# Gate sums over partitions on Pool instead of TensorE, and a changed order on VectorE in the seven-product pairs

## The chip, the cores and the metric

The kernel runs on one core of a Trainium2 chip. The core has TensorE (PE, with its weight loads PEld), VectorE (DVE), ScalarE (ACT), GpSimd (Pool) and SyncE (SP), which here issues the loads; 16 DMA engines move data between HBM and the core's memory. The metric is the device time of one execution in microseconds (us), the median of several runs.

## The reference

One layer of a decoder trunk on 256 tokens of width 2048, all in float32. With x the tokens and c one conditioning vector:

```
shift, scale, gate = split(silu(c) @ ada_w + ada_b, 3)      # each 2048 wide
h = rmsnorm(x, norm_g) * (1 + scale) + shift
b_gate, c_gate, v, g = split(h @ w_in, 4)                   # each 4096 wide
u = causal_depthwise_conv(c_gate * v, conv_w)               # width 3
y = (b_gate * u * silu(g)) @ w_out                          # back to 2048
out = rmsnorm(x + gate * y, final_g)
```

The change is in the gate, a vector-matrix product over 2048 rows of ada_w, and in the last product, with w_out.

## The kernel before, in words

**Precision and loads.** Each weight tile of 128 x 2048 (1 MB) is loaded by SP. ACT casts it to the matrix format (the high part, `hi`, L341), DVE subtracts that from the original (the low part, `lo`, L346), and TensorE makes three products of each pair of operands: hi with hi, hi with lo, lo with hi (L471 for w_in, L695 for w_out). Raw, high and low tiles have three buffers each, which take turns.

**Stages.** First x is turned and normalised. Then blocks of four output tiles of w_in (`part`, `mm_s`) run while the shift and scale are still being made, with an order that a planner (`plan`) fixes. `mixed` does the convolution and the gating for each of four such chunks (L528 to L537). From about 381 us on, the second half of the 4096 columns runs in eight wider blocks (L626, `mm_b`), each of four parts, two tiles to a part. Last come the products with w_out: the first 1024 output columns from 730.79 us (L748, `mm_w` and `mm`), then two blocks of 512 (L790, `mm_o`).

**The gate.** For each of four groups of 512 output columns (`dc`), DVE multiplies 16 tiles of ada_w with silu(c) and accumulates them into `gacc`, 128 partitions by 512 (L591, L593). `gacc` uses the tag `gv`, which has two buffers, so a group takes the buffer of the group two before. At the end of a group a TensorE product with a matrix of ones sums over the partitions and puts the same sum in each (`ps_gate`, L596, float32 in two passes), and DVE adds the bias to it (L597). The bias was loaded into `gate` before (L563). Pieces of the gate are called once for each weight tile of the wide blocks, but with a later priority, so that a scheduler places them where it finds room.

**Token forms and pairs of seven products.** Six of the 16 pairs of row tiles of w_out (`SEVEN`, pairs 10 to 15) are multiplied with seven block products instead of eight, the Strassen-Winograd way. `token_forms` (L604) makes four sums of the blocks of y in a scratch half of `zs[0]` and keeps their high and low parts. `seven` (L713) does the same for the four 512-wide blocks of a raw tile: DVE makes the sums (L720, L722, L723) and the low part of the blocks themselves (L724), ACT casts the blocks (L721) and then the sums (L341), and DVE makes the sums' low part (L346). Between two such pairs stands an ordinary pair of 24 products, since the order of the pairs is (0, 1, 10, 2, 11, 3, 12, 4, 13, 5, 14, 6, 15, 7, 8, 9).

**What sets the order.** Each engine takes its instructions in the order of the built program. A scheduler makes that order from priorities and its own estimates of durations; `later` and `behind` shift or fix places, and `add_manual_dep` with `after` orders two instructions of one engine without a wait.

Of the kernel before, what the change touches and what calls it, by code (L numbers as in the profile page):

```python
# [8 lines left out]
F32 = mybir.dt.float32  # L9
F32R = mybir.dt.float32r  # L10
AF = mybir.ActivationFunctionType
ALU = mybir.AluOpType

P = 128
# [103 lines left out]
def short_conv_layer(ctx: ExitStack, tc: tile.TileContext, x, c, norm_g, ada_w, ada_b, w_in, conv_w, w_out, final_g, out):  # L118
    nc = tc.nc
# [11 lines left out]
    psum = ctx.enter_context(tc.tile_pool(name="psum", bufs=3, space=PSUM))  # L131
# [5 lines left out]
    def slot(shape, name, dtype=F32):  # L137
        return slots.tile(shape, dtype, tag="slot", name=name)
# [6 lines left out]
    def w_tile(kind, name, dtype=F32, i=None):  # L145

        if i is None:
            i = nth[kind] % 3
            nth[kind] += 1
        return wpool.tile([P, SLOT], dtype, tag=f"{kind}{i}", name=name, bufs=1)  # L150
# [12 lines left out]
    after = mybir.DependencyInfo(mybir.DependencyClass.NoSync, mybir.DependencyReason.DATA)  # L163
# [75 lines left out]
    ones = const.tile([P, 1], F32, tag="ones", name="ones")  # L239
# [35 lines left out]
    for t in range(TT):  # L275
        for dh in range(2):
# [3 lines left out]
            else:  # L280
                nc.vector.scalar_tensor_tensor(
                    out=junk[:, t], in0=xt[t][dh], scalar=1.0, in1=xt[t][dh], op0=ALU.mult, op1=ALU.mult,
# [50 lines left out]
    def hi_tile():  # L333
        return w_tile("hi", "hi", F32R)

    def lo_tile(lo_tag="lo"):
        return w_tile(lo_tag, "lo", F32R)
# [23 lines left out]
    def split(raw, n, lo_tag="lo"):  # L361

        return split_lo(raw, n, split_hi(raw, n), lo_tag)
# [64 lines left out]
    sums = {}  # L428
# [132 lines left out]
    zs = [slot([P, 2, 2, T], f"z{j}") for j in range(2)]  # L561
# [6 lines left out]
    def gate(dc):  # L568
        return gates[dc // 2][:, dc % 2, :]

    gate_todo = [(dc, j) for dc in range(4) for j in range(0, KT, 2)]
    gacc = [None]

    def gate_piece():
        if not gate_todo:
            return
        dc, j = gate_todo.pop(0)
        at = adap.tile([P, ASLOT], F32, tag="at", name="at_g", bufs=4)
        at3 = at.rearrange("p (k f) -> p k f", k=2)
        with later(GIVE):  # L580
            gate_sums(dc, j, at3)

    def gate_sums(dc, j, at3):
        nc.sync.dma_start(at3, adas[:, j : j + 2, 2, dc * 512 : (dc + 1) * 512])
        if j == 0:
            gacc[0] = adap.tile([P, 512], F32, tag="gv", name="gacc")
        ga = gacc[0]
        for i in range(2):
            s = silu_c[:, j + i : j + i + 1]
            if j + i == 0:  # L590
                nc.vector.tensor_scalar_mul(ga, at3[:, i, :], s)  # L591
            else:
                nc.vector.scalar_tensor_tensor(out=ga, in0=at3[:, i, :], scalar=s, in1=ga, op0=ALU.mult, op1=ALU.add)  # L593
        if j + 2 == KT:
            ps = psum.tile([P, 512], F32, tag="sm", name="ps_gate", bufs=2)
            nc.tensor.matmul(ps, ones.to_broadcast([P, P]), ga, start=True, stop=True)  # L596
            nc.vector.tensor_tensor(out=gate(dc), in0=ps, in1=gate(dc), op=ALU.add)  # L597

    KP = 8
    EP = 4  # L600
# [2 lines left out]

    def token_forms(pair, u):  # L604

        sums = zs[0][:, 0].rearrange("p a (b f) -> p (a b) f", f=P)
        a11, a12 = u[:, 0, 0:P], u[:, 1, 0:P]
        a21, a22 = u[:, 0, P:T], u[:, 1, P:T]
        s1n, s2, s3, s4 = (sums[:, j] for j in range(4))
        nc.vector.scalar_tensor_tensor(out=s1n, in0=a21, scalar=-1.0, in1=a22, op0=ALU.mult, op1=ALU.subtract)  # L610
        nc.vector.scalar_tensor_tensor(out=s2, in0=s1n, scalar=-1.0, in1=a11, op0=ALU.mult, op1=ALU.subtract)
        nc.vector.tensor_tensor(out=s3, in0=a11, in1=a21, op=ALU.subtract)
        nc.vector.tensor_tensor(out=s4, in0=a12, in1=s2, op=ALU.subtract)
        if pair < 14:
            form = adap.tile([P, ASLOT], F32R, tag="at", name="form", bufs=4).rearrange("p (h s f) -> p h s f", h=2, f=P)
            hi, lo = form[:, 0], form[:, 1]
        elif pair == 14:
            hi, lo = (adap.tile([P, 512], F32R, tag="gv", name="form_g").rearrange("p (s f) -> p s f", f=P) for _ in range(2))
        else:
            form = hpool.tile([P, 2, 4, P], F32R, tag="big2", name="form_h")  # L620
            hi, lo = form[:, 0], form[:, 1]
        forms[pair] = hi, lo
        nc.scalar.copy(hi, sums)
        nc.vector.tensor_tensor(out=lo, in0=sums, in1=hi.bitcast(F32), op=ALU.subtract)

    for ct in range(NS, NCT, 2):  # L626
        for q in QUARTERS:
# [17 lines left out]
            if q == 1:  # L645
                nc.scalar.copy(z, bank)
                zc = z
            elif q == 2:
                nc.vector.tensor_tensor(out=zc, in0=bank, in1=zc, op=ALU.mult)
                for j in range(2):  # L650
                    conv(ct + j, z[:, j, :], zc[:, j, :])
                u = z
            elif q == 3:
                nc.scalar.activation(z, bank, AF.Silu)
                nc.vector.tensor_tensor(out=u, in0=u, in1=z, op=ALU.mult)
            else:
                nc.vector.tensor_tensor(out=u, in0=bank, in1=u, op=ALU.mult)
                split_y(ys[ct // 2], u)
                if ct // 2 in SEVEN:
                    token_forms(ct // 2, u)  # L660
# [28 lines left out]
    def y_parts(ct, t):  # L689
        return [ys[ct // 2][:, ct % 2, h, t * P : (t + 1) * P] for h in range(2)]  # L690

    def triple(dst, y, hi, lo, opens=False, ends=False):

        for i, (a, b) in enumerate(((0, hi), (0, lo), (1, hi))):
            nc.tensor.matmul(dst, y[a], b, start=opens and i == 0, stop=ends and i == 2, skip_group_check=True)  # L695
# [17 lines left out]
    def seven(j, raw):  # L713


        opens, last = j == SEVEN[0], j == SEVEN[-1]
        sums = w_tile("lo", "sums_o")
        hi, lo = hi_tile(), lo_tile("raw")
        b, s, bh, bl = (v.rearrange("p (b f) -> p b f", f=W) for v in (raw, sums, hi, lo))
        nc.vector.tensor_tensor(out=s[:, 0:2], in0=b[:, 1:3], in1=b[:, 0:1].to_broadcast([P, 2, W]), op=ALU.subtract)  # L720
        nc.scalar.copy(bh[:, 1:4], b[:, 1:4])  # L721
        nc.vector.tensor_tensor(out=s[:, 2], in0=b[:, 2], in1=s[:, 0], op=ALU.add)  # L722
        nc.vector.tensor_tensor(out=s[:, 3], in0=b[:, 3], in1=s[:, 2], op=ALU.subtract)  # L723
        nc.vector.tensor_tensor(out=bl[:, 1:4], in0=b[:, 1:4], in1=bh[:, 1:4].bitcast(F32), op=ALU.subtract)  # L724
        sh, sl = (v.rearrange("p (b f) -> p b f", f=W) for v in split(sums, SLOT, "raw"))

        def f(i):
            return [forms[j][h][:, i] for h in range(2)]

        triple(p1, y_parts(2 * j, 0), bh[:, 1], bl[:, 1], opens, last)  # L730
        triple(wide[0][:, 1], y_parts(2 * j + 1, 0), bh[:, 3], bl[:, 3])
        triple(wide[0][:, 0], f(3), bh[:, 2], bl[:, 2])
        triple(p75[:, 0], f(2), sh[:, 1], sl[:, 1], opens, last)
        triple(p75[:, 1], f(0), sh[:, 0], sl[:, 0], opens, last)
        triple(p6, f(1), sh[:, 2], sl[:, 2], opens, last)
        triple(wide[1][:, 1], y_parts(2 * j + 1, 1), sh[:, 3], sl[:, 3])
# [12 lines left out]
    for n, j in enumerate(order):  # L749
        raw = w_tile("lo" if n else "raw", "raw_o")  # L750
        load_o(raw, 2 * j, 2, 0, 2 * W)
        load_ends(n - 4)
        if j in SEVEN:
            seven(j, raw)
            if j == SEVEN[-1]:
                gather()
            continue
        hi, lo = split(raw, SLOT, "raw")
        for t in range(TT):
            for k in range(2):  # L760
                for d in range(2):
                    o = slice((k * 2 + d) * W, (k * 2 + d + 1) * W)
                    triple(
                        wide[t][:, d], y_parts(2 * j + k, t), hi[:, o], lo[:, o],
                        n == 0 and k == 0, j == order[-1] and k == 1,
                    )
# [24 lines left out]
    for dc in range(2, 4):  # L791
# [16 lines left out]
        for ep in range(n_ep):  # L808
# [3 lines left out]
            if dc == 3:  # L812
# [3 lines left out]
                    out=raw3, in0=raw3, in1=gate(dc).unsqueeze(1).to_broadcast([P, EP, W]), op=ALU.mult  # L816
# [8 lines left out]
        for t in range(TT):  # L825
# [4 lines left out]
            if dc == 2:  # L830
                gated(t, dc * W, W, po[t], pr, 1)
                ps = part_sum[:, t : t + 1]
# [29 lines left out]
```

## Time and profile before

| | us |
|---|---|
| median of 3 runs | 911.48 (911.47 to 912.15) |
| the profiled execution | 911.95 |
| its span, first to last instruction | 910.2 |
| granted TensorE clock, mean | 0.997 of full speed |

The profiled execution is one run of its own; what lies between its time and its span is before the first and after the last instruction. Durations in the next parts come from it. In the lines of the profile, `out<-in` are the program's names, `xN` a count, and a number in brackets the idle time of the engine ahead of the instruction with what ended it. "hi L341 <- PE mm_b: 154.0, 46, 4.4" in a list of waits reads: waited for that, 154.0 us in total, 46 times, 4.4 us at the longest. A DMA's line gives its count, size and the us from issue to landing. In a table by stretches, x counts instructions.

### The profile page before, as it was taken

The numbers are of one execution on the slowest core, as the hardware profiler recorded it, in microseconds if no ns is written. First come the engines' busy times: TensorE is split into PE (matmuls) and PEld (weight loads), VectorE is DVE, ScalarE is ACT, GpSimd is POOL, SyncE is SP. The second block draws the span as 40 slices with busy tenths as digits, with TensorE's granted clock in tenths as the row PEclk, the third lists the DMA queues.
The fourth block names the chain that finished last, engine by engine and source line by source line (L and its number), as shares of the span: only waits on it lengthen the run. The fifth ranks groups of instructions, "written<-read, shape, count | busy, mean of one in ns | idle before, by whom it ended". The sixth has DMA issues, their size and how long they took to land.

```text
span 910.2 us, 16272 instructions
## 1 busy us (share of the span) xinstructions
PE 894.2 (98%) x7029; PEld 854.7 (94%) x7029; DVE 653.5 (72%) x647; ACT 476.1 (52%) x422; POOL 0.7 (0%) x6
## 2 busy tenths in 40 slices
PE   6999999999999999999999999999999999999996
PEld 4999999999999999999999999999999987788885
DVE  4889899889888886665555686555555577887882
ACT  6768866665558765643333434343444335544343
POOL 0000000000000000000000000000000000000000
PEclk9999999999999999999999999999999999999998
DMA  9999999999998686676666887656666486685542
GB/s 313 367 371 349 364 309 365 346 370 359 345 327 282 184 301 189 189 241 202 202 186 186 259 273 231 201 185 194 185 193 197 137 307 191 209 293 185 185 138 93
DMA packets 159656, 227.65 MB, mean 250 GB/s; under 512 B 5680, under 2 KB 104160, under 8 KB 159200
## 3 DMA queue, kind: packets, MB, share of 16 engines
q1 hardware_dynamic: 159456, 226.56, 75.7%
q8 instruction: 55, 0.90, 0.4%
q14 instruction: 17, 0.14, 0.0%
q10 hardware_dynamic: 128, 0.04, 0.0%
HBM read 224.49 MB, written 2.10 MB: 249 GB/s over the span
## 4 chain that ended last, share of the span: by engine, by line
PE 98%; ACT 1%; DMA 1%; ACTq 0%; issue 0%; DVE 0%
PE mm_b L471 38%; PE mm_s L471 38%; PE mm_o L695 10%; PE mm_w L695 7%; PE mm L695 2%; PE tp_idle L258 1%; DMA rows<-in_ada_b_dram 1%; PE sum L380 1%; PE ps_gate L596 0%; PE tp_g L461 0%; PE tp_x L310 0%; ACT hi L341 0%; ACT acc L492 0%; ACT hT L327 0%; ACT mm_s L504 0%; ACT big L787 0%
## 5 line engine op out<-in xcount | busy, mean ns | idle before, releaser
L471 PE MATMUL mm_s<-hT,hi 128*128 128x256 f32 x2048 | 350.4, 277 | 0.1
L471 PE MATMUL mm_b<-hT,hi 128*128 128x256 f32 x2048 | 349.4, 276 | 0.0
L471 PEld LDWEIGHTS mm_s<-hT,hi 128*128 128x128 f32 x2048 | 308.5, 188 | 1.0 <-ACT hT L327 0.3
L471 PEld LDWEIGHTS mm_b<-hT,hi 128*128 128x128 f32 x2048 | 308.2, 188 | 0.5 <-issue 0.5
L471 PE MATMUL mm_b<-hT,lo 128*128 128x256 f32 x1024 | 282.6, 276 | 0.0
L471 PE MATMUL mm_s<-hT,lo 128*128 128x256 f32 x1024 | 282.2, 277 | 0.0
L346 DVE TENSOR_TENSOR lo<-raw,hi 128x2048 fp32r<-128x2048 f32 (+1 forms) x66 | 148.0, 2243 | 113.6 <-ACT hi L341 113.2
L341 ACT CAST hi<-raw 128x2048 fp32r<-128x2048 f32 (+1 forms) x66 | 123.7, 1874 | 193.9 <-PE mm_b L471 152.6
L471 PEld LDWEIGHTS mm_b<-hT,lo 128*128 128x128 f32 x1024 | 192.2, 188 | 0.5 <-issue 0.5
L471 PEld LDWEIGHTS mm_s<-hT,lo 128*128 128x128 f32 x1024 | 191.7, 188 | 0.3 <-DVE lo L346 0.2
L346 DVE TENSOR_TENSOR lo<-raw_s,hi 128x2048 fp32r<-128x2048 f32 (+1 forms) x80 | 147.6, 1850 | 32.8 <-ACT hi L341 32.0
L341 ACT CAST hi<-raw_s 128x2048 fp32r<-128x2048 f32 (+1 forms) x80 | 124.0, 1559 | 72.9 <-PE mm_s L471 59.6
L454 DVE SCALAR_TENSOR_TENSOR gv<-at,silu_c,gv 128x512 f32<-128x512 f32 x105 | 78.6, 749 | 6.3 <-DMA at<-in_ada_w_dram 4.5
L341 ACT CAST hi<-raw_o 128x2048 fp32r<-128x2048 f32 x26 | 49.6, 1906 | 60.6 <-PE mm_o L695 36.6
L695 PE MATMUL mm_o<-hi,y 128*128 128x512 f32 x256 | 78.7, 389 | 0.0
L346 DVE TENSOR_TENSOR lo<-raw_o,hi 128x2048 fp32r<-128x2048 f32 x26 | 59.5, 2290 | 24.2 <-ACT hi L341 24.1
L492 ACT COPY acc<-mm_s 128x1024 f32<-128x1024 f32 x54 | 54.6, 1012 | 34.7 <-PE mm_s L471 34.7
L695 PE MATMUL mm_w<-hi,y 128*128 128x512 f32 x184 | 58.2, 390 | 0.0
L695 PEld LDWEIGHTS mm_o<-hi,y 128*128 128x128 f32 x256 | 48.0, 188 | 9.9
L695 PE MATMUL mm_o<-lo,y 128*128 128x512 f32 x128 | 49.5, 389 | 0.0
L593 DVE SCALAR_TENSOR_TENSOR gacc<-at_g,silu_c,gacc 128x512 f32<-128x512 f32 x60 | 45.0, 749 | 5.6 <-DMA at_g<-in_ada_w_dram 4.6
L695 PEld LDWEIGHTS mm_w<-hi,y 128*128 128x128 f32 x184 | 34.5, 188 | 7.7 <-ACT hi L341 0.2
(142 smaller groups left out, 512.6 us busy)
## 6 DMA issues: line engine op xcount, KB each, us to landing
raw<-in_sc_w_in_dram SPq DMA_DIRECT2D x64, 1024.0 KB, 5.6
raw_s<-in_sc_w_in_dram SPq DMA_DIRECT2D x47, 1024.0 KB, 8.5
raw_o<-in_sc_w_out_dram SPq DMA_DIRECT2D x32, 1024.0 KB, 5.1
at<-in_ada_w_dram SPq DMA_DIRECT2D x114, 256.0 KB, 8.4
raw_s<-in_sc_w_in_dram SPq DMA_DIRECT2D x33, 512.0 KB, 6.9
at_g<-in_ada_w_dram SPq DMA_DIRECT2D x32, 512.0 KB, 7.6
at<-in_ada_w_dram SPq DMA_DIRECT2D x6, 512.0 KB, 9.4
x<-in_x_dram SPq DMA_DIRECT2D x4, 512.0 KB, 6.1
```

The source lines that it names most:

```text
L258: nc.tensor.matmul(tp_idle, ident, ones[:, 0:1].to_broadcast([P, 512]), start=True, stop=True)
L341: nc.scalar.copy(hi[:, :n], raw[:, :n])
L346: nc.vector.tensor_tensor(out=lo[:, :n], in0=raw[:, :n], in1=hi[:, :n].bitcast(F32), op=ALU.subtract)
L380: nc.tensor.matmul(sums0[:, o * P : (o + 1) * P], rows[:, o // NK0, (o % NK0) * P : (o % NK0 + 1) * P], col.to_broadcast([P, P]), start=k ...
L454: nc.vector.scalar_tensor_tensor(out=gv, in0=at4[:, i], scalar=c_k, in1=gv, op0=ALU.mult, op1=ALU.add)
L471: mm = last_mm[0] = nc.tensor.matmul(dst, w, h[k], start=begins and left, stop=ends, skip_group_check=True)
L492: nc.scalar.copy(acc[ch, q], bank)
L593: nc.vector.scalar_tensor_tensor(out=ga, in0=at3[:, i, :], scalar=s, in1=ga, op0=ALU.mult, op1=ALU.add)
L695: nc.tensor.matmul(dst, y[a], b, start=opens and i == 0, stop=ends and i == 2, skip_group_check=True)
```

## The change

The product with ones and the addition behind it go. In their place Pool makes the sums over partitions in seven steps, with a shift `away` of 64, 32, 16, 8, 4, 2 and 1 partitions. In each step two DMAs that Pool issues copy `gacc`, turned around by `away` partitions, into `turned`, and Pool adds the copy to `gacc`. After the seven steps each partition holds the sum of all 128; Pool then adds the bias. `turned` is the first half of `zs[0]`, which held the sums of `token_forms`; these move to the second half, which also holds the block's first part.

In `seven`, the low part of the raw blocks is ordered behind the fourth sum on DVE.

```diff
     gate_todo = [(dc, j) for dc in range(4) for j in range(0, KT, 2)]
     gacc = [None]
+    turned = zs[0][:, 0].rearrange("p a f -> p (a f)")
...
         if j + 2 == KT:
-            ps = psum.tile([P, 512], F32, tag="sm", name="ps_gate", bufs=2)
-            nc.tensor.matmul(ps, ones.to_broadcast([P, P]), ga, start=True, stop=True)
-            nc.vector.tensor_tensor(out=gate(dc), in0=ps, in1=gate(dc), op=ALU.add)
+            away = 64
+            while away:
+                nc.gpsimd.dma_start(turned[0 : P - away], ga[away:P])
+                nc.gpsimd.dma_start(turned[P - away : P], ga[0:away])
+                nc.gpsimd.tensor_tensor(out=ga, in0=ga, in1=turned, op=ALU.add)
+                away //= 2
+            nc.gpsimd.tensor_tensor(out=gate(dc), in0=ga, in1=gate(dc), op=ALU.add)
...
-        sums = zs[0][:, 0].rearrange("p a (b f) -> p (a b) f", f=P)
+        sums = zs[0][:, 1].rearrange("p a (b f) -> p (a b) f", f=P)
...
-        nc.vector.tensor_tensor(out=s[:, 3], in0=b[:, 3], in1=s[:, 2], op=ALU.subtract)
-        nc.vector.tensor_tensor(out=bl[:, 1:4], in0=b[:, 1:4], in1=bh[:, 1:4].bitcast(F32), op=ALU.subtract)
+        all_sums = nc.vector.tensor_tensor(out=s[:, 3], in0=b[:, 3], in1=s[:, 2], op=ALU.subtract)
+        low = nc.vector.tensor_tensor(out=bl[:, 1:4], in0=b[:, 1:4], in1=bh[:, 1:4].bitcast(F32), op=ALU.subtract)
+        tc.add_manual_dep(low.ins, all_sums.ins.name, after, reason="the sums' cast runs beside the low part")
```

In the changed file the lines behind the first edit stand one to six further down: the gate's products are at L592 and L594, Pool's transfers at L598 and L599, its additions at L600 and L602; in `seven` the sums are at L725, L727 and L728, the cast at L726 and the low part at L729.

## The prediction

> **What bounds the kernel now.** I read the profile page first, its busy line and its chain of work that ended last; then the chain in order of time; then who waits for whom; then the timelines of the two stages that the change touches.
>
> ```profile
> PE 894.2 (98%) x7029; PEld 854.7 (94%) x7029; DVE 653.5 (72%) x647; ACT 476.1 (52%) x422; POOL 0.7 (0%) x6
> ...
> PE 98%; ACT 1%; DMA 1%; ACTq 0%; issue 0%; DVE 0%
> ```
>
> Busy time alone would prove little, but the chain agrees: 98% of the span is a chain of TensorE work. The other engines have room, Pool nearly all of it. So a TensorE instruction that goes is worth its full time, wherever the next product's operands are early. The waits of ACT between 400 and 730 us say that they are:
>
> ```profile
> ACT hi L341 <- PE mm_b L471: 154.0, 46, 4.4
> ```
>
> ACT waits 154.0 us in 46 places for TensorE to give back a buffer; no row of that view has it wait for a weight load. The chain in order of time (start, length, what) shows the sums that go, and the rate of the 512-column products:
>
> ```profile
> 302.94 1.72 PE ps_gate L596 x4
> ...
> 541.79 0.86 PE ps_gate L596 x2
> ...
> 586.20 0.86 PE ps_gate L596 x2
> ...
> 730.79 10.89 PE mm_w L695 x48
> ...
> 815.93 86.83 PE mm_o L695 x383
> ```
>
> All four sums stand on the chain, in two passes each. An undisturbed product takes 86.83 / 383 = 0.2267 us. The stage of the output's first half is the one place where TensorE is slower than that:
>
> ```profile
> 730.79:815.93 85.14, 85.11 (x368) 68.23 (x368) 66.95 (x52) 40.31 (x25) 0.00 (x0) 1.00 0.71 247
> ...
> PEld mm L695 <- DVE lo L346: 1.4, 4, 0.3
> PEld mm L695 <- ACT hi L721: 1.1, 4, 0.3
> ```
>
> The first row is the busy time of each engine in that stretch (PE, PEld, DVE, ACT, POOL, then the granted clock, 1.00, and DMA). The code has ten ordinary pairs of 24 products there and six seven-product pairs of 21, 366, and one hoisted from the next stage: 367 x 0.2267 = 83.20. So 85.14 - 83.20 = 1.94 us are lost, with weight loads waiting four times each for a low part and for a block's cast.
>
> **Part 1, the gate's sums.** Removed: 8 passes of TensorE on the chain, 1.72 + 0.86 + 0.86 = 3.44 us, and four additions on DVE that are off the chain. It would be less if the products behind a sum found their operands late once they come that much sooner; it cannot be more. How early operands are is in these rows (DVE's low part, ACT's casts):
>
> ```profile
> 437.17 2.29 DVE L346 TENSOR_TENSOR lo<-raw,hi 128x2048 fp32r<-128x2048 f32 x1 [3.15 <-ACT hi L341]
> ...
> 446.06 1.91 ACT L341 CAST hi<-raw 128x2048 fp32r<-128x2048 f32 x1 [3.53 <-PE mm_b L471]
> ...
> 451.54 1.92 ACT L341 CAST hi<-raw 128x2048 fp32r<-128x2048 f32 x1 [2.77 <-issue]
> ```
>
> The low part that ends at 439.46 belongs to the tile that TensorE begins when it gives a buffer back at 446.06: 6.6 us early, so I take all 3.44. The raw buffer free at 439.46 is cast again, three tiles on, at 451.54: 12.1 us for a load.
>
> Added: for each of four columns seven steps of two Pool DMAs and one Pool addition, then the gate's addition: 56 DMAs, 32 Pool instructions. Nothing else stands on Pool behind its 6 instructions of setup, so its waits queue only its own chain. The question is who waits for Pool. In the built program that is DVE's first product of the third and of the fourth column (L592 of the changed file: its accumulator is the buffer of two columns before) and, far later, the forms of pair 14. The third column's products have moved on DVE behind the first wide block's split at L424, the fourth's stand where they stood; four 0.5 MB loads move with them on SP, past some twenty weight loads and the gate's two bias loads, into a stage with time to spare on DVE (20.21 of 40 us busy) and on the DMA engines (0.63). The rows give the deadlines:
>
> ```profile
> 440.00:480.00 40.00, 40.00 (x356) 40.00 (x355) 20.21 (x15) 16.46 (x12) 0.00 (x0) 1.00 0.63 191
> ...
> 315.92 0.69 DVE L535 TENSOR_TENSOR acc<-acc,acc 128x512 f32<-128x512 f32 x1
> ...
> 396.10 1.29 DVE L597 TENSOR_TENSOR gate<-ps_gate,gate 128x512 f32<-128x512 f32 x2 [4.44 <-DMA gate<-in_ada_b_dram]
> ...
> 428.46 0.68 DVE L424 TENSOR_TENSOR y<-z,y 128x512 fp32r<-128x512 f32 x1
> ...
> 519.19 0.49 DVE L591 TENSOR_SCALAR gacc<-at_g,silu_c 128x512 f32<-128x512 f32 x1 [2.40 <-DMA at_g<-in_ada_w_dram]
> ...
> L593 DVE SCALAR_TENSOR_TENSOR gacc<-at_g,silu_c,gacc x60: 743/751/754, 223.7 to 545.4; 128x512 f32<-128x512 f32 x60
> ...
> L623 ACT CAST form_g<-z x1: 616/616/616, 689.5 to 689.5; 128x512 fp32r<-128x512 f32 x1
> ```
>
> The first column's chain starts when L535 frees the slot that holds the turned copy, about 316 us; its last addition needs the gate's bias, landed at 396.1. It must be done by 429: 113 us for seven steps, 16 us each. The second runs from 397 to a deadline of 519: 17 us a step. The fourth starts when its products end, about 546, and must give its buffer to a form of pair 14 at 689: 20 us a step. A step is not in the trace; the nearest rows bound it:
>
> ```profile
> 1.01 0.29 POOL masks.py:199 TENSOR_SCALAR_AFFINE_SELECT ident<-ident 128x128 f32<-128x128 f32 x1
> ...
> rows<-in_c_dram ACTq DMA_DIRECT2D x1, 8.0 KB, 3.2
> ...
> gate<-in_ada_b_dram SPq DMA_DIRECT2D x2, 512.0 KB, 10.9
> ```
>
> Pool's 128 columns in 0.29 us make 512 in 1.2 us; a DMA lands after 3.2 us at the least and 10.9 at the most. So a step lies between 4.4 and 12.1 us, and I take 6, as its transfers (at most 254 KB) are nearer to the small one. Seven take 42, at most 85 us: in time, and the gate itself is first used behind 815.93. Cost on the chain: 0. If that cover is gone, it is rival B.
>
> The Trainium skill speaks against this in "SBUF — State Buffer", section "Who interferes with whom": a DVE instruction with two SBUF inputs and a GpSimd instruction that reads SBUF exclude each other, and the later one waits for all of the other. No row of this profile can show that, since Pool is idle beside DVE. By it, an addition would hold up a low part by its own length; by the Pool row that is 1.2 us against the 6.6 of slack, so the sum stays the same, but a step grows.
>
> Also hidden: the forms' sums move to the half of the buffer that ACT overwrites for the next block; ACT and DVE have read it by then in their own order, two casts ahead.
>
> **Part 2, the low part behind the fourth sum.** One period of DVE (start, length) and its ACT partner:
>
> ```profile
> 756.59 1.22 DVE L720 TENSOR_TENSOR sums_o<-raw_o 128x1024 f32<-128x1024 f32 x1
> 757.72 1.75 DVE L724 TENSOR_TENSOR lo<-raw_o,hi 128x1536 fp32r<-128x1536 f32 x1
> 759.39 0.69 DVE L722 TENSOR_TENSOR sums_o<-raw_o,sums_o 128x512 f32<-128x512 f32 x1
> 760.11 0.69 DVE L723 TENSOR_TENSOR sums_o<-raw_o,sums_o 128x512 f32<-128x512 f32 x1
> 762.85 2.29 DVE L346 TENSOR_TENSOR lo<-sums_o,hi 128x2048 fp32r<-128x2048 f32 x1 [2.05 <-ACT hi L341]
> 765.06 2.29 DVE L346 TENSOR_TENSOR lo<-raw_o,hi 128x2048 fp32r<-128x2048 f32 x1
> 767.26 1.22 DVE L720 TENSOR_TENSOR sums_o<-raw_o 128x1024 f32<-128x1024 f32 x1
> ...
> 760.91 1.91 ACT L341 CAST hi<-sums_o 128x2048 fp32r<-128x2048 f32 x1 [4.05 <-DVE sums_o L723]
> ...
> 766.11 1.48 ACT L721 CAST hi<-raw_o 128x1536 fp32r<-128x1536 f32 x1 [1.49 <-DMA raw_o<-in_sc_w_out_dram]
> ```
>
> From L720 to L720 DVE takes 767.26 - 756.59 = 10.67 us, 2.05 of them idle until ACT has cast the sums. TensorE needs for the same two pairs 45 x 0.2267 = 10.20. So DVE, though busy only 79% of the stage, sets the pace: 0.47 us a period, four periods, 1.9 us. That is the 1.94 again.
>
> Now the 1.75 us of L724 move behind L723, into the 2.05 us of idleness. DVE's period becomes 10.67 - 1.67 = 9.0. What is late next? The load: the raw block is read last by L724, then at 1.13 + 0.72 + 0.72 + 1.75 = 4.3 us after L720; from the block's release to the next cast it was 766.11 - 760.80 = 5.3; together 9.6 us. ACT's three casts take 1.91 + 1.90 + 1.48 = 5.3. All are below 10.20, so TensorE becomes the bound. The block's low part is ready 4.3 us after L720, at 756.59 + 4.3 = 760.9, and the chain has its product at 762.65, so that this is early too:
>
> ```profile
> 762.65 0.45 PE mm L695 x2
> ```
>
> In the built program four pairs also have their first product, which waited for L721, some 23 places later. Gain between 0 (the load binds after all) and 1.94; I take 1.9, as each loop above has 0.6 us to spare.
>
> **The sum.** 3.44 + 1.9 = 5.34 us. The profiled execution took 911.95 us, of which the span is 910.2; it would take 906.6. The median is 911.48, 0.47 below it: **906.1 us**.
>
> **Rivals.**
> A. Only the TensorE passes count: the stage stays at 85.1 us because the load is the loop. For it: ACT waits 1.49 us for the load in the row above. Against: that wait ends before DVE is free, and 9.6 < 10.20. Time 911.48 - 3.44 = 908.0.
>
> B. Slower: Pool's chain is late. Place: DVE's first product of the third column, with the low parts of the weight tiles queued behind it, and TensorE behind those. It decides from 16 us a step; every microsecond beyond the 6.6 of slack costs one. At 20 us a step the chain ends at 456, 27 us late: 906.1 + 27 - 6.6 = 927. Against it: the slowest row gives 12.1. For it: two Pool DMAs per step, of a kind that no row shows.
>
> C. Slower too: the transfers hold up weight loads. A raw load moves 1 MB in the page's 5.6 us:
>
> ```profile
> raw<-in_sc_w_in_dram SPq DMA_DIRECT2D x64, 1024.0 KB, 5.6
> ```
>
> On 16 engines that is 64 KB each; the last step's 127 rows of 2 KB, if one engine carried them alone, would take 4 x 5.6 = 22 us there. Alternating with it, a load lands 5.6 us later, and 12.1 - 5.6 = 6.5 are free: nothing lost. At twice that delay it is 4.7 us late, in each of four columns: 906.1 + 19 = 925. The Trainium skill, "DMA: Bandwidth & Descriptors", section "Why a DMA increments its semaphore by 16 and not by 1", says that a transfer of 127 partitions can fall to a single engine, with an exception for some GpSimd copies.
>
> That the change does not do what it says is all but excluded: in the built order the fourth sum precedes the low part in all six pairs, and no product ps_gate is left.
>
> **How the numbers follow.** Forecast 0.70; A 0.12; B 0.06; C 0.05; small leftovers of B and C, a few microseconds that eat the gain, 0.07. The bound for same is 0.2%, 1.8 us, about what a measurement of this kernel can tell from no change. Forecast and A are faster, with 0.02 of the leftovers: 0.84. The rest of the leftovers is same: 0.05. B and C are slower: 0.11. The range holds the forecast and A: from 906.1 less 0.7, the spread of the runs before, to A plus 1.2 for small waits: 905.4 to 909.2.
>
> **What would show it.** Right: no ps_gate on the chain; Pool with some 38 instructions and steps of 4.4 to 12 us; no wait of DVE for Pool at L592; the seven-product stage 83.2 us; DVE's idle time before the sums' low part 0.3 us; no weight load waiting for L346 or L726. Wrong: that stage at 85 us (A), a gap in TensorE at about 429 or 519 us (B), ACT waiting for raw loads while Pool's transfers run (C).

## The result and the profile after

The changed kernel takes **906.57 us** (median of six runs, 906.15 to 907.16); the kernel before, run beside it, 911.52 (911.32 to 912.84). The ratio is 0.994, 95% interval 0.993 to 0.9951. The profiled execution took 906.51 us with a span of 904.7, that is 5.44 us less than the one of before; the prediction's sum was 5.34. Between the medians it is 4.95 us.

First the page of the changed kernel, its busy line and its chain by engine:

```profile
PE 888.5 (98%) x7021; PEld 853.6 (94%) x7021; DVE 662.0 (73%) x643; ACT 476.7 (53%) x422; POOL 81.5 (9%) x94
...
PE 97%; ACT 1%; DMA 1%; ACTq 0%; issue 0%; DVE 0%
```

TensorE has eight instructions fewer, and Pool has 94: 56 transfers that it issues, and 38 others (28 additions of the steps, four of the bias, six of the setup). DVE is busy for 8.5 us longer though it has four additions fewer. The chain is still TensorE. In the same chain in order of time (start, length, what) no sum is left:

```profile
231.94 146.81 PE mm_s L471 x1295
378.75 348.16 PE mm_b L471 x3072
726.91 10.89 PE mm_w L700 x48
...
809.94 87.05 PE mm_o L700 x384
```

The 3072 products of the wide blocks are now one unbroken piece. From stage to stage the time went as follows. The output's first half starts at 726.91 instead of 730.79, 3.88 us earlier; 0.35 of that is there before the first sum (the long run of `mm_s` begins at 231.94 instead of 232.29; nothing of the change lies before it), which leaves 3.53 for the four sums, where 3.44 was predicted. The stage itself:

```profile
726.91:809.94 83.03, 83.03 (x368) 68.70 (x367) 67.84 (x52) 40.84 (x25) 0.00 (x0) 1.00 0.72 253
```

It lasts 83.03 us for 366 products (the 367th is no longer hoisted from the next stage: `mm_o` counts 384 instead of 383), and TensorE is busy for all of it. 85.14 - 83.03 = 2.11, less 0.23 for the hoisted product: 1.88 gained, where 1.9 was predicted. Behind the stage 0.26 us come back, beside the hoisted product. That is the stretch behind the last product with w_out, 7.71 us instead of 7.44; it varies by as much between executions (7.53 us in the kernel with the gate alone and 7.85 in the one with the order alone, both further down), so neither it nor the 0.35 is put down to the change. 0.35 + 3.53 + 1.88 - 0.26 = 5.5, the difference of the spans.

One period of DVE and its partner ACT in that stage:

```profile
752.24 1.22 DVE L725 TENSOR_TENSOR sums_o<-raw_o 128x1024 f32<-128x1024 f32 x1
753.49 0.69 DVE L727 TENSOR_TENSOR sums_o<-raw_o,sums_o 128x512 f32<-128x512 f32 x1
754.22 0.69 DVE L728 TENSOR_TENSOR sums_o<-raw_o,sums_o 128x512 f32<-128x512 f32 x1
754.83 1.75 DVE L729 TENSOR_TENSOR lo<-raw_o,hi 128x1536 fp32r<-128x1536 f32 x1
756.96 2.29 DVE L346 TENSOR_TENSOR lo<-sums_o,hi 128x2048 fp32r<-128x2048 f32 x1 [0.38 <-ACT hi L341]
760.23 2.29 DVE L346 TENSOR_TENSOR lo<-raw_o,hi 128x2048 fp32r<-128x2048 f32 x1 [0.98 <-ACT hi L341]
762.44 1.22 DVE L725 TENSOR_TENSOR sums_o<-raw_o 128x1024 f32<-128x1024 f32 x1
```

```profile
755.02 1.91 ACT L341 CAST hi<-sums_o 128x2048 fp32r<-128x2048 f32 x1 [2.03 <-DVE sums_o L728]
```

The cast of the sums (755.02 to 756.93) now lies beside the low part of L729, and DVE's idle time ahead of the sums' low part is 0.38 us instead of 2.05. The period is 762.44 - 752.24 = 10.20, which is TensorE's own 45 x 0.2267: DVE now idles 0.98 us for a cast of ACT, which in turn waited 1.37 us for TensorE to give back a buffer. The prediction had 9.0 for DVE alone, and DVE does wait 1.36 of its 10.20.

Pool's side, by groups (count, busy us and mean ns, idle time and what ended it), and its transfers by size (count, KB, us to landing):

```profile
L600 POOL TENSOR_TENSOR gacc<-gacc,z 128x512 f32<-128x512 f32 x28 | 43.0, 1534 | 108.7 <-DMA z<-gacc 108.7
```

```profile
z<-gacc POOLq DMA_DIRECT2D x8, 128.0 KB, 5.1
z<-gacc POOLq DMA_DIRECT2D x4, 254.0 KB, 3.9
...
z<-gacc POOLq DMA_DIRECT2D x4, 192.0 KB, 5.9
...
z<-gacc POOLq DMA_DIRECT2D x4, 2.0 KB, 3.5
```

An addition takes 1.53 us in the mean, and Pool waits 108.7 / 28 = 3.9 us a step for its transfers. In the list of waits nothing outside Pool waits for Pool, so the whole chain is covered. The third column's chain ends here; the long idle time behind it is the wait for the fourth column's products:

```profile
500.25 1.29 POOL L602 TENSOR_TENSOR gate<-gacc,gate 128x512 f32<-128x512 f32 x1
544.42 0.56 POOL L598 DMA_DIRECT2D z<-gacc  x1 [42.88 <-DVE gacc L594]
```

### The profile page after: what moved, and what is told of

It reads as the page before. It is cut to its first block, busy times and chain, and to the rows that moved or that the text cites. A ratio compares the mean times of both kernels' runs of the same rounds, so it can differ in the third digit from the quotient of the medians.

```text
span 904.7 us, 16406 instructions
## 1 busy us (share of the span) xinstructions
PE 888.5 (98%) x7021; PEld 853.6 (94%) x7021; DVE 662.0 (73%) x643; ACT 476.7 (53%) x422; POOL 81.5 (9%) x94
## 4 chain that ended last, share of the span: by engine, by line
PE 97%; ACT 1%; DMA 1%; ACTq 0%; issue 0%; DVE 0%
PE mm_b L471 38%; PE mm_s L471 38%; PE mm_o L700 10%; PE mm_w L700 7%; PE mm L700 2%; PE tp_idle L258 1%; DMA rows<-in_ada_b_dram 1%; PE sum L380 1%; PE tp_g L461 0%; PE tp_x L310 0%; ACT hi L341 0%; ACT acc L492 0%; ACT hT L327 0%; ACT mm_s L504 0%; ACT big L793 0%; ACT z L842 0%
## 5 line engine op out<-in xcount | busy, mean ns | idle before, releaser
L346 DVE TENSOR_TENSOR lo<-raw,hi 128x2048 fp32r<-128x2048 f32 (+1 forms) x66 | 152.4, 2310 | 104.2 <-ACT hi L341 103.7
L600 POOL TENSOR_TENSOR gacc<-gacc,z 128x512 f32<-128x512 f32 x28 | 43.0, 1534 | 108.7 <-DMA z<-gacc 108.7
L594 DVE SCALAR_TENSOR_TENSOR gacc<-at_g,silu_c,gacc 128x512 f32<-128x512 f32 x60 | 46.9, 782 | 5.6 <-DMA at_g<-in_ada_w_dram 4.5
L598 POOL DMA_DIRECT2D z<-gacc x28 | 15.6, 557 | 376.6 <-DVE acc L535 310.5
```

Source lines behind the costliest of these rows:

```text
L346: nc.vector.tensor_tensor(out=lo[:, :n], in0=raw[:, :n], in1=hi[:, :n].bitcast(F32), op=ALU.subtract)
L598: nc.gpsimd.dma_start(turned[0 : P - away], ga[away:P])
L600: nc.gpsimd.tensor_tensor(out=ga, in0=ga, in1=turned, op=ALU.add)
```

## The experiments

Every time below is the median of a kernel's runs, with the ratio to the kernel before on the same chip and its 95% interval, if not said otherwise.

### One part at a time

**The gate alone**: the changed kernel without its last line.

```diff
-        tc.add_manual_dep(low.ins, all_sums.ins.name, after, reason="the sums' cast runs beside the low part")
```

> The changed kernel without the dependency in the seven-product pairs: the gate's sums on Pool, the low part of the blocks back ahead of the third sum on DVE. My theory: the gate's part is worth the 3.44 us of TensorE passes, so 911.5 - 3.4 = 908.1 us, and the seven-product stage takes 85.1 us again with weight loads waiting for the sums' low part. Rival (the order in the pairs is what the whole gain hangs on, the gate's part gives little): 910 to 911.5. Rival (the gate's part gives all): 906.6.

Measured: 908.20 (908.01 to 909.15), 0.9965 [0.9953, 0.9978]. Its stage lasts as long as before:

```profile
726.69:811.84 85.15, 85.07 (x368) 68.28 (x368) 66.94 (x52) 40.32 (x25) 0.00 (x0) 1.00 0.72 247
```

**The order alone**: the kernel before with the last edit of the diff and nothing else.

> The kernel before with only the dependency: low part of the blocks behind the fourth sum, the gate's sums on TensorE. My theory: DVE's period falls from 10.67 to below 10.2 us, TensorE sets the pace, 911.5 - 1.9 = 909.6 us, stage 83.2 us. Rival (the stage is bound by the load of the raw block, or the gain needs the gate's part): 911.5, stage 85.1.

Measured: 910.30 (909.92 to 910.88), 0.9984 [0.9976, 0.9993]. The four sums are on its chain again, and its stage is the changed kernel's:

```profile
730.77:813.80 83.03, 83.03 (x367) 68.69 (x367) 67.95 (x52) 40.86 (x25) 0.00 (x0) 1.00 0.73 253
```

Against the 911.82 of that group of runs the gate gives 3.6 us and the order 1.5; together 5.1, against 4.95 for both. The parts add up, and neither hides the other. In the traces the order's part of the stage is 1.88 us, and the medians show a little less of it.

**The product put back**: the changed kernel, Pool's chain and all, with the product with ones issued again and its result not used.

```diff
+            ps = psum.tile([P, 512], F32, tag="sm", name="ps_gate", bufs=2)
+            nc.tensor.matmul(ps, ones.to_broadcast([P, P]), ga, start=True, stop=True)
             away = 64
```

> The changed kernel with the TensorE product with ones put back once per column; nothing reads its result, the gate still comes from Pool. My theory (the gate's part is worth the TensorE passes and nothing else): 906.6 + 3.4 = 910.0 us, with eight passes at L596 or so on the chain. Rival (the gain came from what DVE and the scheduler were freed of: four additions and the third column's place): 906.6 us.

Measured: 910.18 (909.97 to 910.84), 0.9983 [0.9974, 0.9991]: 3.6 us over the changed kernel, with Pool's 28 steps still made. The product also holds back Pool's third chain, whose first addition waits 81.2 us for it, but no weight load of the wide blocks waits for a low part in this trace. So the gate's gain is those eight passes on TensorE, and not that DVE lost its additions.

### Why the order gains

**The first product held back.** The change also moves the first product of four pairs some 23 places back on TensorE, and a rival was that this order was the gain. Here the kernel before has only that: the first product is ordered behind the ordinary pair, DVE stays as it was.

```diff
+        first = triple(p1, y_parts(2 * j, 0), bh[:, 1], bl[:, 1], opens, last)[0]
+        tc.add_manual_dep(first.ins, ordinary[0].ins.name, after, reason="behind the ordinary pair")
```

> The kernel before, with DVE's order in the pairs as it was, but each seven-product pair's first TensorE product ordered behind the ordinary pair ahead of it, as it stands in the changed kernel. My theory (DVE's period of 10.67 us is the bound): 911.5 us, stage 85 us, the waits of weight loads for the block's cast L721 go, and those for DVE's low parts grow by as much. Rival (the product that stood some 23 places ahead and waited for L721 was the loss, DVE's order is beside the point): 909.6 us, stage 83.2 us.

Measured: 912.21 (910.88 to 912.63), 1.0003 [0.9994, 1.0012]. Waits of TensorE's weight loads in it:

```profile
PEld mm L695 <- DVE lo L346: 1.3, 4, 0.3
PEld mm_w L695 <- ACT hi L341: 1.1, 4, 0.3
```

The wait for L721 is gone, but another one of the same 1.1 us stands in its place, and the stage lasts 85.13 us. So the waits were symptoms: the order of the products decides where TensorE waits, and not how long.

**The low part one place further.** L729 goes behind the sums' low part instead of behind the fourth sum.

```diff
+        low = nc.vector.tensor_tensor(out=bl[:, 1:4], in0=b[:, 1:4], in1=bh[:, 1:4].bitcast(F32), op=ALU.subtract)
+        tc.add_manual_dep(low.ins, sums_low[0].ins.name, after, reason="behind the sums' low part")
```

> The changed kernel with the low part of the blocks moved one place further, behind the sums' low part. My theory: DVE stands idle again for the 2 us of the sums' cast and its period is 10.67 us again, so the stage takes 85 us or more and the time is 908.5 (908 to 910, since the block's low part is also later for its product). Rival (all that matters is that the fourth sum comes early): 906.6 us, stage 83.1 us.

Measured: 929.53 (926.35 to 929.87), 1.0184 [1.017, 1.0198]. **A miss**: slower than before by 18 us. DVE's period and its waits for loads show the cause:

```profile
758.16 1.23 DVE L727 TENSOR_TENSOR sums_o<-raw_o 128x1024 f32<-128x1024 f32 x1 [3.31 <-DMA raw_o<-in_sc_w_out_dram]
...
762.86 2.29 DVE L348 TENSOR_TENSOR lo<-sums_o,hi 128x2048 fp32r<-128x2048 f32 x1 [2.02 <-ACT hi L341]
765.07 1.75 DVE L732 TENSOR_TENSOR lo<-raw_o,hi 128x1536 fp32r<-128x1536 f32 x1
766.74 2.28 DVE L348 TENSOR_TENSOR lo<-raw_o,hi 128x2048 fp32r<-128x2048 f32 x1
772.18 1.23 DVE L727 TENSOR_TENSOR sums_o<-raw_o 128x1024 f32<-128x1024 f32 x1 [3.16 <-DMA raw_o<-in_sc_w_out_dram]
```

The low part is the last reader of the raw block, and the next load needs the block. It is released at 766.82, 8.7 us after L727, and the load lands in time for 772.18, 5.4 us later: a loop of 14.0 us against TensorE's 10.20, in the prediction's terms 4.3 + 5.3 = 9.6 become 8.7 + 5.4. Five such periods cost 19 of the 23 us that lie between this kernel and the changed one; the granted clock, 0.92 in this stage behind TensorE's gaps, adds to it. So the load loop is real, and it has room for the place that the change chose, but not for the next one.

### How much room Pool's chain has

**Four more additions a step**, whose results go to the slot that the next step overwrites.

```diff
                 nc.gpsimd.tensor_tensor(out=ga, in0=ga, in1=turned, op=ALU.add)
+                for _ in range(4):
+                    nc.gpsimd.tensor_tensor(out=turned, in0=ga, in1=turned, op=ALU.add)
```

> The changed kernel with four more Pool additions in each step, into the copy that the next step overwrites (112 more in all; the gate is the same). A step grows from about 6.7 to some 12 us. My theory (DVE's low parts are 6.6 us early, so that Pool may hold them up): the low parts that meet an addition take up to 3.4 us in place of 2.29, DVE's busy time grows by 10 to 40 us, and the time stays at 906.6. Rival (the exclusion of Pool and DVE already costs the chain something): 908 or more, in proportion to the additions.

Measured: 939.5 (935.38 to 943.6), 1.032 [1.0299, 1.0341]. **A miss**, by 33 us. Its waits:

```profile
DVE form_g L631 <- POOL z L602: 21.0, 1, 21.0
ACT z L653 <- DVE form_g L631: 18.6, 1, 18.6
...
PEld mm_b L471 <- DVE lo L346: 11.7, 9, 3.2
...
PEld mm_b L471 <- ACT z L653: 10.4, 1, 10.4
```

Two things were wrong. The chain was late: 28 steps from 312 to 739 us make 15 each instead of the 12 expected, and DVE waited 21.0 us for it at pair 14's form (`form_g`, which takes a buffer of `gacc`). The prediction's deadline of 16 us a step was that of the third column, which DVE would reach first. But in the builds with a much longer Pool chain the third and fourth column's products stand later on DVE: they begin at 468 and 555 us here and at 461 and 538 in the next kernel, where they begin at 427 and 517 in the changed kernel. Their chains move with them, and all four have to end by the form of pair 14, about 689 us where TensorE is not held up: (689 - 312) / 28 = 13.5 us a step. And low parts were late, in nine places, before that; DVE's busy time grew by 80.6 us (742.6 against 662.0), not by 10 to 40. On top comes the clock. The gap, and the stretch behind it (the granted clock is the third number from the end):

```profile
730.00:740.00 10.00, 0.05 (x1) 0.00 (x0) 1.14 (x2) 0.41 (x1) 7.47 (x6) 0.68 0.34 106
740.00:750.00 10.00, 8.98 (x51) 8.69 (x52) 8.91 (x9) 5.33 (x7) 0.00 (x0) 0.64 0.01 2
```

In the second stretch TensorE is busy 8.98 us with 51 products, where the stretch from 720 to 730 us held 89.

**Each transfer twice** (the inner two lines in a loop of two).

```diff
+                for _ in range(2):
+                    nc.gpsimd.dma_start(turned[0 : P - away], ga[away:P])
+                    nc.gpsimd.dma_start(turned[P - away : P], ga[0:away])
```

> The changed kernel with each of Pool's transfers made twice in a row (112 in place of 56; the second copy writes the same). A step takes about 11 us, the four columns' chains end near 390, 471, 548 and 625 us. My theory: all ahead of whoever waits (DVE for the third column near 455, the forms of pair 14 at 686 to 690), so 906.6 us. Rival (the transfers take time from the weight loads): each adds as much again as the first 56 cost, 907.5 or more, with ACT waiting for raw loads.

Measured: 910.64, with runs from 906.69 to 915.11, 0.9984 [0.9966, 1.0002], so as a time it can't be told from the kernel before. A step took 13 to 15 us instead of the 11 expected, about the edge of 13.5 from above, and the trace shows this edge. Pool's last addition, the instruction that waits for it, and the chain behind it:

```profile
698.15 1.28 POOL L603 TENSOR_TENSOR gate<-gacc,gate 128x512 f32<-128x512 f32 x1
```

```profile
699.47 0.69 DVE L630 TENSOR_TENSOR form_g<-z,form_g 128x512 fp32r<-128x512 f32 x1 [9.96 <-POOL gate L603]
```

```profile
701.12 1.26 DVE lo L346
...
702.42 27.28 PE mm_b L471 x238
```

Pool ends at 699.4, 10 us behind the time at which DVE reached the form; the low part of a weight tile is queued behind that form, and TensorE waits 1.3 us for it: rival B of the prediction, at another place. This is the trace of the run of 910.03 us; what the slower runs waited for is not shown.

**Each transfer three times**, one run.

> The same with each transfer made three times. A step takes about 15.5 us, a column 108; the scheduler has put the third and fourth column's products later on DVE, so the first deadline holds (420 us against 470). The fourth column's chain ends near 744, and DVE's low part of pair 14's form, due at 690, waits for its buffer. My theory: slower by about 50 us (940 to 975), one gap in TensorE at some 697 us, behind a DVE instruction that waits for Pool. Rival (Pool's chain is off the path however long, as nothing reads the gate before 810 us): 906.6.

Measured: 984.99. The direction held, the size was larger than expected. Pool's transfers are 40% of the chain that ended last, a step takes (800.1 - 312) / 28 = 17.4 us, DVE waits for it at the same form, ACT for DVE, and TensorE's weight load for ACT:

```profile
PEld mm_w L701 <- ACT z L652: 40.2, 1, 40.2
...
DVE form_g L630 <- POOL gate L603: 39.4, 1, 39.4
...
PEld mm_b L471 <- ACT z L652: 21.6, 1, 21.6
...
ACT form L629 <- DVE gacc L594: 17.6, 1, 17.6
```

That is one gap and not all of the loss. The last two lines are a second one, from 599 to 620 us, that was not foretold: an earlier pair's form has its buffer among those of the ada_w tiles (`at`), so its cast waited for the fourth column's products, which begin only at 603 us in this build.

The granted clock was 0.963 in the mean, and 0.50 in the stretches from 605 to 620 and from 770 to 800 us in which TensorE stood still.

### What an addition on Pool costs DVE

**One more addition a step.** With it the chain should be in time, so this asks about the additions themselves.

```diff
+                nc.gpsimd.tensor_tensor(out=turned, in0=ga, in1=turned, op=ALU.add)
```

> The changed kernel with one more Pool addition behind each of the 28 steps (its result goes to the slot that the next step overwrites, so the output is the reference's). A step grows from 6.2-7.5 us by 1.3 us, or by up to 3.4 where a low part is in the way: at most 11, so the four chains still end in time, and only the exclusion between Pool's additions and DVE's low parts is doubled. Theory: a single addition makes a low part at most 1.1 us longer, against some 6 us of slack, so nothing: 906.6 (905.9 to 907.5), and no wait of TensorE for the low part at L346. Rival: it was the additions between the low parts, and not the late chain, that cost 11.7 us of weight-load waits in nine places with four more additions a step; with one more, a quarter of that: 909.5.

Measured: 909.39 (906.58 to 911.94 in twelve runs), 0.9977 [0.9965, 0.9989]. That is the rival's number, not the theory's. Pool's last gate addition ends at 617 us, so the end of the chain holds nothing up; but the chain that ended last leaves TensorE at 520.78 and comes back to it at 539.32:

```profile
523.30 0.56 DVE lo L346
...
526.60 0.75 DVE gacc L594
...
527.37 8.85 DMA at_g<-in_ada_w_dram
...
536.98 2.30 DVE lo L346
...
539.32 190.75 PE mm_b L471 x1678
```

Here a product of the fourth column (L594) was late behind a low part of 3.38 us, so the buffer for a 0.5 MB load was free late, so the next product was, and with it the low part behind it. The same 30 us of both kernels (busy us of PE, PEld, DVE, ACT, POOL), the changed one first:

```profile
519.00:549.00 30.00, 30.00 (x267) 30.00 (x266) 25.39 (x26) 13.05 (x10) 2.02 (x3) 1.00 0.84 268
```

```profile
519.00:549.00 30.00, 28.40 (x248) 28.01 (x247) 26.24 (x25) 11.36 (x9) 10.01 (x7) 1.00 0.88 281
```

In the changed kernel DVE is busy 85% of this stretch and Pool has one addition in it, at its end; the third column's chain ended at 501.5, before the fourth column's products began at 517. With the longer steps that chain ended at 535.7 and stood beside them. Three more kernels ask whether it is that place.

**Each transfer twice, but once in the fourth column.**

```diff
+                for _ in range(2 if dc < 3 else 1):
```

> The changed kernel with each turning transfer made twice in the first three columns, but once in the fourth (the output is the reference's). With all four doubled the last addition ended at 699.5 us and DVE waited 10.0 us for it at pair 14's form; the runs lay between 906.7 and 915.1. Theory: the transfers cost nothing of themselves, and that kernel stood at the edge of its deadline. Without the doubling in the fourth column the chain ends some 7 x 6 = 40 us earlier, and the time is 906.6 (906.0 to 907.6) in all runs. Rival: the added traffic holds up weight loads; three quarters of the traffic is left, and so three quarters of the loss and the scatter: median near 909.5, runs up to 912.

Measured: 907.14, 0.9955 [0.9943, 0.9967]; five of six runs from 906.48 to 907.22, one, the profiled one, at 910.61. Mostly the theory: without the late end the loss and most of the scatter are gone, though seven eighths of all the transfers are left. The run of 910.61 has one wait of 2.5 us of TensorE for a low part, in the fourth column's products again, beside the third column's longer chain.

**One more addition a step, but none in the third column; and two more in the third column alone.** The edits, one each:

```diff
+                for _ in range(dc != 2):
+                for _ in range(2 * (dc == 2)):
```

> As the run with one more Pool addition a step, but none in the third column: 21 additions more instead of 28 (the output is the reference's). In that run the third column's chain ended at 535.7 us instead of 501.5, beside the fourth column's products on DVE (519 to 551), and TensorE waited there for a low part behind a product whose 0.5 MB load had come late. Theory: what cost 2.8 us is that place alone, where DVE has products, low parts and no spare time; so without the third column's extra additions the time is 906.6 (906.1 to 907.5) and the runs don't scatter. Rival: every added addition costs a little wherever it stands, three quarters of 2.8: 908.7, with runs up to 911.

> The counterpart: two more Pool additions a step in the third column alone, 14 in all, and none elsewhere (the output is the reference's). Its chain, 456 to 501.5 us in the changed kernel, grows by some 4 us a step to about 530 and runs beside the fourth column's products. Theory: that place costs 2 to 5 us: median 908.5 to 911.5, with runs that scatter from 906.6 to 912, and a wait of TensorE for a low part between 517 and 560 us. Rival (every addition costs the same wherever it stands): half of 2.8, 908.0.

Measured: 907.17, 0.996 [0.9948, 0.9972], five of six runs within 906.74 to 908.08, one at 910.55; and 911.14 (908.64 to 913.41 in twelve runs), 0.9995 [0.9985, 1.0004]. Against the changed kernel's 906.57, 21 additions elsewhere cost 0.6 us, no more than the spread of its runs; 14 in the third column cost 4.6, nearly the whole gain of the change. The same stretch in the two kernels, the one without and the one with them:

```profile
519.00:549.00 30.00, 30.00 (x267) 30.00 (x266) 26.24 (x27) 12.97 (x10) 1.09 (x2) 1.00 0.93 298
```

```profile
519.00:549.00 30.00, 28.48 (x252) 28.28 (x250) 27.89 (x24) 12.91 (x10) 12.75 (x9) 1.00 0.85 264
```

DVE is busy 27.89 of 30 us in the second and gets 24 instructions done instead of 27, beside 12.75 us of Pool instead of 1.09. So the place decides, and the number counts there: 28 additions of which seven stand in the third column cost 2.8 us, 14 there cost 4.6. What stays open is why single runs of the kernels with added work reach 910.5 and others do not; there is no trace of a good and a bad run of one kernel.

## Why the prediction was right, point by point

- **The sums' 3.44 us.** Right: 3.53 between the traces, 3.6 us between the medians in the kernel with the gate alone, and 3.6 lost again when the product came back.
- **Pool's chain is hidden.** Right for this kernel. The step was taken as 6 us between 4.4 and 12.1; the chains took 7.5, 6.2, 6.3 and 7.0 us a step. The transfers landed after 3.2 to 5.9 us, in the median of each size, near the small load, as chosen; but not because they are small, since 254 KB took 3.9 us and 2 KB 3.5. The 3.2 us was not the least either: single transfers of Pool landed after 2.5 to 7.9 us. And the sum of a step left out the 1.1 us in which Pool issues its two transfers.
- **The deadlines of 16, 17 and 20 us a step.** Too wide, and with them the reason why B was unlikely; the change did not need them, as its steps stay well below. What a longer chain meets first is not a waiting DVE but a busy one: the third column's chain should end before the fourth column's products start, (517 - 456) / 7 = 8.7 us a step. That edge is soft. In the kernel with each transfer twice but once in the fourth column, that chain also runs beside those products, with one addition in some 15 us, and five of six runs stay near 907; with three additions in 12 us (two more in the third column) all twelve are above 908.6. Behind that comes pair 14's form at some 13.5. The price of B, one us per us, was too small as well: at 17.4 us a step the time is 985, and 927 was the price for 20, as the forms, the reordered columns and the clock come on top.
- **Additions on Pool beside DVE.** The prediction took 1.2 us for an addition, and a low part that is held up by as much. Two lines of the changed kernel's time line for Pool, and two for DVE:

```profile
341.92 1.30 POOL L600 TENSOR_TENSOR gacc<-gacc,z 128x512 f32<-128x512 f32 x1 [4.18 <-DMA z<-gacc]
...
348.03 3.39 POOL L600 TENSOR_TENSOR gacc<-gacc,z 128x512 f32<-128x512 f32 x1 [3.50 <-DMA z<-gacc]
```

```profile
342.55 2.82 DVE L346 TENSOR_TENSOR lo<-raw_s,hi 128x2048 fp32r<-128x2048 f32 x1 [0.95 <-ACT hi L341]
...
347.98 2.29 DVE L346 TENSOR_TENSOR lo<-raw_s,hi 128x2048 fp32r<-128x2048 f32 x1 [2.62 <-ACT hi L341]
```

  The addition that starts first takes its 1.30 us, and the low part that starts within it, with 0.67 us of the addition to go, takes 2.82 instead of 2.29. Where the low part starts first, at 347.98, the addition takes 3.39; with 2.24 us of the low part to go, that leaves 1.15 for itself. That agrees with the rule of the Trainium skill that the prediction weighed ("SBUF — State Buffer", section "Who interferes with whom"): the later of the two waits for all of the other. The slack does take it up in the changed kernel; in the fourth column's 30 us it doesn't, once Pool's additions move there. The 6.6 us had been read at 440 us, where DVE is busy for 20.21 of 40 us, and were used for the whole kernel; around the fourth column's products the kernel before already shows 33.33 of 40 (the third busy time in the row):

```profile
520.00:560.00 40.00, 40.00 (x350) 39.52 (x349) 33.33 (x36) 16.24 (x13) 0.00 (x0) 1.00 0.87 278
```

- **Part 2.** Right in mechanism and size: 1.88 us for 1.9, with TensorE as the bound. 0.3 us of idle time was foretold ahead of the sums' low part, and it is 0.38. The kernel with the first product held back speaks for DVE's period against the order of the products, and the one with the low part one place further shows that the load loop of 9.6 us was no idle worry.
- **Rival A** (only the passes count) is the kernel with the gate alone: 908.2 for 908.0. It is what the change would have been without its second part.
- **Rival C** fell on its premise. 127 rows land after 3.9 us, not 22, and raw loads 0.3 us later than before (5.9 instead of 5.6), well inside the 6.5 that were free. Of the two cases in the Trainium skill's "DMA: Bandwidth & Descriptors", section "Why a DMA increments its semaphore by 16 and not by 1", the landing time agrees with the exception for some GpSimd copies, not with the single engine. Which engines moved the rows is not in the profile.

## What to carry to other kernels

Taking work off the engine that sets the end is worth that work's full time even if the replacement takes fifty times as long, as long as it ends before anyone asks for it and nothing on the path runs late beside it; here 3.5 us of TensorE became some 190 us of a chain on Pool. Before trusting such a cover, look not only for who waits at its end, but for what the new work runs beside: an engine that is 85% busy in that stretch may have no room for a neighbour that blocks it. When an instruction is moved into an idle gap, count the loop through the buffer that it releases: one place further cost 23 us.

## What the runs showed of the hardware

- DVE's accumulating products of 512 columns, 0.75 us in the median, took up to 1.8 us beside Pool's additions, and even the plain product with a scalar (0.48 us) took 1.4 to 1.5 us in four of the kernels with added work, each time beside an addition; it has one large input only.
- In a 10 us gap of TensorE the granted clock was 0.68 and in the 10 us behind it 0.64 (four more additions); in the gaps of 20 and 40 us of the kernel with each transfer three times it fell to 0.50. So a gap costs more than its length: in the kernel with four more additions the waits for low parts and for ACT's copy add up to 11.7 + 10.4 = 22.1 us, and TensorE reached the output 28.4 us later (755.31 against 726.91), though it began the wide blocks at the same time (378.4 against 378.6). The slower products fit the rest: 51 of them took 8.98 us behind the gap, where 10 us held 89 before it.
- A transfer that Pool issues between partitions kept Pool itself busy for 0.50 to 0.70 us: 0.55 in the median for those of 128 to 254 KB, 0.51 for those of 2 to 128 KB.
